# Where the tail of each stage is issued: merging the last four gated tiles together, deferring the first convolutions, and the last norm's factor in PSUM

## The chip, the cores and the metric

The kernel runs on one core of a Trainium2 chip. Its engines work from separate in-order queues: PE (TensorE) multiplies matrices into PSUM, DVE (VectorE) and ACT (ScalarE) do elementwise work, POOL (GpSimd) a little of it, and SP and ACT issue the DMAs. The metric is the device time of one execution in microseconds (us).

## The reference

One layer of a decoder trunk, 1024 tokens of 1024 channels, float32. What matters here:

```python
u = _modulate(h, g_mix, sh1, sc1)                 # RMSNorm, scale, shift; sh, sc, gt from silu(c) @ w_ada
y_att, y_ssm = ...                                # windowed attention and S5 branch, each projected to 1024
merged = sigmoid(g_att + gb_att) * y_att + sigmoid(g_ssm + gb_ssm) * y_ssm
h = h + gt1 * (merged @ w_out)
u = _modulate(h, g_ffn, sh2, sc2)
a, val = split(u @ w_up)                          # 2 x 2048 channels
conv = b_conv + sum(w_conv[j] * shift(a, j) for j in range(3))
h = h + gt2 * ((silu(conv) * val) @ w_down)
return _rmsnorm(h, g_final)
```

## The kernel before

Activations lie channels by tokens in tiles of 128 channels; the tokens fall in two halves (hf 0 and 1) of 512. Every matrix operand is kept as a high part in the PE's fast float format and a low part (the rest): ACT copies the high part, DVE (or POOL) subtracts to get the low part, and each product is three matmuls of 128x512 (`mm3`). A "group" is one output tile of 128x512: 8 k-tiles, 24 matmuls, for a contraction over 1024 channels; 2 k-tiles, 6 matmuls, for the projection of the S5 branch.

The order of work is written by a Python builder that keeps a clock of its own. Each k-tile calls `unit(0.65)`, which advances that clock and resumes background generators (`spawn`) that are due; what they issue then goes onto the engines' queues at that place. `drain()` runs background generators to their end, one after the other. So the builder's clock sets only the order on each queue; the chip sets the times.

The merge stage follows `merge_order`: "g" items are the gates of the S5 branch (two groups of 24 matmuls over u, then a sigmoid on ACT, L737), "p" items project two tiles (four groups of 6 matmuls, PSUM tags "s" and "t" of two banks each) and merge them on DVE: multiply by the gate (L757), add the attention part (L758), ACT's high part (L759), and the low part (L762), which is issued one group later through `lows`. Meanwhile `gen_ada` loads 16 rows of w_ada on ACT's queue (L772) and reduces each with a dot product on DVE (L1459), three buffers in turn. Ahead of the last "p" item the builder drains it. `Weights` loads and splits the next weights (L118 on ACT, L121 on DVE) into one of two `whl` buffers or, for some of the later ones, into the big pool A of 17 tiles, in which u, the gates and the merged tiles live too. A pool's tile is free when the last instruction that reads it is done.

Then w_out is multiplied (8 groups per half, `residual` adds to h, L882, and gathers the squares for the norm). The up projection's first pair of tiles is done as plain groups (8 groups: kind 0 the convolved part, kind 1 the value part, e = 0 in tag "s", e = 1 in tag "mm"); the rest of the up projection and the down projection are Strassen products M1 to M7 of 12 matmuls (L1305). During those first groups `gen_u2b` norms the second half of the tokens (L897, L902, L865, L869) and forms the differences T1, T2, T3, T4 of the quarters (L937 to L940). `block` takes a group's result: for kind 0 ACT scales it (L1015) and DVE adds the two shifted copies (L1022) and the edge (L1010); for kind 1 DVE multiplies (L1004).

At the end each half's last norm is a generator `final`: PE sums the squares (L1418, L1420), ACT (L1427, L1429) and DVE (L1431, L1432) form the factor in `acc`, and DVE (L1405, L1407) and POOL (L1407) multiply the eight tiles by it; SP stores them (L1409, L1412). The second half comes in two pieces of 256 tokens.

Of the kernel before, what the change touches and what calls it, by code (L numbers as in the profile page):

```python
# [10 lines left out]
F32 = mybir.dt.float32  # L11
# [30 lines left out]
ADA1 = 8.0  # L42
FIN = 5.0
PREP = 4
# [25 lines left out]
class Weights:  # L70
# [25 lines left out]
    def _split_to(self, n):  # L96
        b, nc = self.b, self.b.nc
        while self.ns < min(n, len(self.items)):
            self.finish()
            self._load_to(self.ns + 1)  # L100
            cols = self.items[self.ns][1]
            raw = self.raw.pop(self.ns)
            if self.ns >= self.small and ((self.ns - self.small) % 3 == 0 or self.wide + 2 <= self.ns < self.wide + 4 or
                                          self.ns >= len(self.items) - 2):
# [38 lines left out]
class Builder:  # L143
# [65 lines left out]
def body(tc, I, O, dbg=None):  # L209
    b = Builder(tc, I, O)  # L210
    nc = tc.nc
    with ExitStack() as ctx:
# [516 lines left out]
        def gate_ssm(m, wg):  # L729
            if m % 2 == 0:  # L730
                page = b.A([P, 2, S], F32, "sg")
                sgs[m], sgs[m + 1] = page[:, 0], page[:, 1]
            sig = sgs[m]
            for hf in range(2):
                ps = b.ps("mm")
                b.run(b.group(ps, wg, KT, U, hf))
                nc.scalar.activation(sig[:, hf * HF:(hf + 1) * HF], ps, AF.Sigmoid,  # L737
                                     bias=cols[:, C_BGATE + KT + m:C_BGATE + KT + m + 1])

# [4 lines left out]

        def proj_ssm(m0, wp, more):

            for e in range(2):
                merged.append(b.A([P, 2, S], R32, "merged"))
            for hf in range(2):
                hs = slice(hf * HF, (hf + 1) * HF)  # L750
                for e in range(2):
                    m = m0 + e
# [4 lines left out]
                    nc.vector.tensor_mul(t, ps, t)  # L757
                    nc.vector.tensor_add(t, t, Tm[m // 2][:, m % 2, hs])  # L758
                    nc.scalar.activation(mt[:, 0, hs], t, AF.Copy)  # L759
# [4 lines left out]
            del sgs[m0], sgs[m0 + 1]  # L764

# [39 lines left out]
        for n, it in enumerate(merge_order):  # L805
# [112 lines left out]
        def gen_u2b():  # L918

            v = nc.vector  # L920
            hs = halves[1]
# [5 lines left out]
            op_new("22")  # L927
            x11, x12, x21, x22 = [[X[q, e][:, k] for k in range(4)] for q in range(2) for e in range(2)]
            xs2 = [("12", k, x12[k]) for k in range(4)] + [("22", k, x22[k]) for k in range(4)]
            for n in range(KT + LAG2):  # L930
# [4 lines left out]
            op_new("T2")  # L935
            for k in range(4):
                v.tensor_sub(x11[k], x12[k], x11[k])  # L937
                v.tensor_sub(x12[k], x22[k], x12[k])
# [57 lines left out]
        def block(r, kind, e, hf, src):  # L996

            m = r + e * FT // 2
            c = page[r][:, e, halves[hf]]
            if kind == 1:  # L1000
                if r:
                    shifted.append(lambda: nc.vector.tensor_mul(c, src, c))
                else:
                    nc.vector.tensor_mul(c, src, c)  # L1004
                return
# [384 lines left out]
        assert not early and not lag and not older  # L1390
        b.drain()


def final(b, hv, hf, acc, ends, hs, cols, O):
    nc = b.nc
    rms_of(b, acc[:, hs], ends.pop(hs.start))
    yield 0.5
    cs = slice(hs.start - hf * HF, hs.stop - hf * HF)
    for m0 in (6, 0, 2, 4):
        out = b.A([P, 2, 256], F32, "out") if hf else None  # L1400
        for m in (m0 + 1, m0):
            x = hv[m, hf][:, cs]
            o = out[:, m - m0] if hf else x
            if m == KT - 1 or hf and m == ND - 1:
                nc.vector.scalar_tensor_tensor(o, x, cols[:, C_GFIN + m:C_GFIN + m + 1], acc[:, hs], op0=OP.mult, op1=OP.mult)  # L1405
            else:
                (nc.gpsimd if m in FPOOL[hf] else nc.vector).tensor_mul(o, x, acc[:, hs])  # L1407
# [15 lines left out]

def rsqrt_of(b, r, ps):

# [5 lines left out]
    nc.vector.scalar_tensor_tensor(t, ps, -EPS * D, t, op0=OP.add, op1=OP.mult)  # L1431
    nc.vector.scalar_tensor_tensor(r, t, 1.5, r, op0=OP.add, op1=OP.mult)  # L1432

# [512 lines left out]
```

## Time and profile before

| | |
|---|---|
| time, median of 3 runs | 1157.44 us (1157.3 to 1157.76) |
| the profiled execution | 1157.34 us, span from first to last instruction 1155.4 us |
| mean granted PE clock | 0.986 |
| busy: PE, DVE, ACT, POOL | 96%, 76%, 50%, 13% of the span |

In the rows below, a timeline row gives start, duration, engine, line and operation, output and inputs, the count of merged instructions, and in brackets the idle time before it with what ended it. A row of a list of waits gives the total, the number and the longest. A row of windows gives start:end and length, busy time and count of PE, PE's weight load, DVE, ACT and POOL, then the granted clock of PE, the share of the DMA engines and GB/s.

### The profile page before, as it was taken

The numbers are of one execution on the slowest core, as the hardware profiler recorded it, in microseconds if no ns is written. First come the engines' busy times: TensorE is split into PE (matmuls) and PEld (weight loads), VectorE is DVE, ScalarE is ACT, GpSimd is POOL, SyncE is SP. The second block draws the span as 40 slices with busy tenths as digits, with TensorE's granted clock in tenths as the row PEclk, the third lists the DMA queues.
The fourth block names the chain that finished last, engine by engine and source line by source line (L and its number), as shares of the span: only waits on it lengthen the run. The fifth ranks groups of instructions, "written<-read, shape, count | busy, mean of one in ns | idle before, by whom it ended". The sixth has DMA issues, their size and how long they took to land.

```text
span 1155.4 us, 14755 instructions
## 1 busy us (share of the span) xinstructions
PE 1112.6 (96%) x5286; PEld 917.2 (79%) x5286; DVE 872.6 (76%) x1672; ACT 581.8 (50%) x1062; POOL 150.2 (13%) x171
## 2 busy tenths in 40 slices
PE   9899999999999999999799998999999999999995
PEld 8677888888878887888688886788888888887884
DVE  6678687876568597378767779888877768889777
ACT  3648777778732312242334565452445346736653
POOL 1001444545421312000000000000000000000003
PEclk9899999999999999999899999999999999999997
DMA  9811111111022221146592342255424337779333
GB/s 370 343 55 70 49 38 37 56 37 65 17 75 73 57 87 51 64 140 195 166 381 81 120 201 73 91 175 190 143 76 146 109 109 272 257 293 343 129 126 146
DMA packets 57337, 159.20 MB, mean 138 GB/s; under 512 B 7440, under 2 KB 13712, under 8 KB 55472
## 3 DMA queue, kind: packets, MB, share of 16 engines
q1 hardware_dynamic: 47520, 144.56, 35.1%
q10 hardware_dynamic: 9744, 13.70, 3.7%
q8 instruction: 41, 0.67, 0.2%
q14 instruction: 32, 0.26, 0.1%
HBM read 126.20 MB, written 31.46 MB: 136 GB/s over the span
## 4 chain that ended last, share of the span: by engine, by line
PE 66%; DVE 15%; ACT 8%; DMA 7%; issue 3%; POOL 0%; SPq 0%; DVEq 0%; ACTq 0%
PE ps_s L1305 13%; PE ps_mm L1305 10%; PE ps_t L1305 8%; PE ps_mm L184 6%; PE ps_mm L185 6%; PE ps_mm L186 6%; PE ps_s L186 3%; PE ps_s L184 3%; PE ps_s L185 3%; DMA xn<-in_xn 2%; PE ps_t L1598 2%; PE ps_s L1562 1%; PE ps_o L1615 1%; PE ps_s L1563 1%; DMA wraw<-in_w 1%
## 5 line engine op out<-in xcount | busy, mean ns | idle before, releaser
L1305 PE MATMUL ps_s<-op,half 128*128 128x512 f32 x792 | 189.5, 390 | 3.0 <-ACT ps_s L1319 2.4
L1305 PEld LDWEIGHTS ps_s<-op,half 128*128 128x128 f32 x792 | 148.4, 188 | 35.4 <-ACT ps_s L1319 3.8
L184 PE MATMUL ps_mm<-u,whl 128*128 128x512 f32 x360 | 145.0, 403 | 3.1 <-ACT sg L737 2.0
L186 PE MATMUL ps_mm<-u,whl 128*128 128x512 f32 x360 | 141.6, 393 | 0.0
L185 PE MATMUL ps_mm<-u,whl 128*128 128x512 f32 x360 | 141.4, 393 | 0.0
L1305 PE MATMUL ps_mm<-op,half 128*128 128x512 f32 x528 | 126.9, 393 | 3.0 <-DVE f L1010 2.8
L1305 PEld LDWEIGHTS ps_mm<-op,half 128*128 128x128 f32 x528 | 99.7, 189 | 24.6 <-ACT half L1110 3.2
L1305 PE MATMUL ps_t<-op,half 128*128 128x512 f32 x432 | 103.9, 390 | 0.7 <-ACT tp L1313 0.7
L1305 PEld LDWEIGHTS ps_t<-op,half 128*128 128x128 f32 x432 | 81.0, 188 | 17.9 <-ACT tp L1313 1.1
L1407 POOL TENSOR_TENSOR hh<-hh,acc 128x512 f32<-128x512 f32 x3 | 4.2, 1439 | 652.1 <-DVE acc L1432 652.1
L121 POOL TENSOR_TENSOR whl<-wraw,whl 128x256 fp32r<-128x256 f32 (+2 forms) x52 | 62.0, 1193 | 207.8 <-ACT whl L118 207.8
L184 PEld LDWEIGHTS ps_mm<-u,whl 128*128 128x128 f32 x360 | 68.1, 189 | 15.3 <-ACT sg L737 2.5
L186 PEld LDWEIGHTS ps_mm<-u,whl 128*128 128x128 f32 x360 | 68.0, 189 | 15.3 <-DVE whl L121 0.3
L185 PEld LDWEIGHTS ps_mm<-u,whl 128*128 128x128 f32 x360 | 68.3, 190 | 10.5
L1603 DVE TENSOR_TENSOR PT<-ps_t,PT 128x512 fp32r<-128x512 f32 (+1 forms) x80 | 50.6, 633 | 28.2 <-ACT PT L1601 27.7
L1111 DVE TENSOR_TENSOR half<-scr,half 128x512 fp32r<-128x512 f32 x80 | 54.5, 685 | 16.2 <-ACT half L1110 16.1
L118 ACT ACTIVATE whl<-wraw 128x256 fp32r<-128x256 f32 (+2 forms) x73 | 49.7, 681 | 28.3 <-PE ps_s L186 14.6
L1574 ACT ACTIVATE S<-S,mcol 128x128 f32<-128x128 f32 (+3 forms) x64 | 49.3, 771 | 14.5 <-DVE mcol L1572 13.0
L1578 POOL TENSOR_SCALAR S<-S,mcol 128x128 f32<-128x128 f32 (+3 forms) x64 | 48.6, 761 | 49.9 <-DVE mcol L1577 35.9
L1110 ACT ACTIVATE half<-scr 128x512 fp32r<-128x512 f32 x80 | 49.0, 626 | 8.6 <-DVE scr L1092 5.5
L1111 DVE TENSOR_TENSOR half<-wraw,half 128x512 fp32r<-128x512 f32 x66 | 45.0, 686 | 7.6 <-ACT half L1110 7.5
L1601 ACT ACTIVATE PT<-ps_t 128x512 fp32r<-128x512 f32 (+1 forms) x80 | 43.7, 550 | 10.4 <-PE ps_t L1598 9.3
(507 smaller groups left out, 2438.0 us busy)
## 6 DMA issues: line engine op xcount, KB each, us to landing
wraw<-in_wup SPq DMA_DIRECT2D x32, 512.0 KB, 3.7
fq<-f SPq DMA_DIRECT2D x16, 1024.0 KB, 5.4
ft<-fq SPq DMA_DIRECT2D x14, 1024.0 KB, 7.5
ada<-in_wada SPq DMA_DIRECT2D x24, 512.0 KB, 8.7
wraw<-in_wdn SPq DMA_DIRECT2D x20, 512.0 KB, 5.9
adaB<-in_wada ACTq DMA_DIRECT2D x16, 512.0 KB, 4.9
wraw<-in_wout SPq DMA_DIRECT2D x16, 512.0 KB, 3.9
hd<-h SPq DMA_DIRECT2D x12, 512.0 KB, 7.9
```

Source lines behind the costliest of these rows:

```text
L118: nc.scalar.activation(w[:, 0, cs], raw[:, cs], AF.Copy)
L121: lo.tensor_sub(w[:, 1, cs], raw[:, cs], w[:, 0, cs].bitcast(F32))
L184: nc.tensor.matmul(ps, wh, xh, start=first, stop=False)
L185: nc.tensor.matmul(ps, wh, xl, start=False, stop=False)
L186: nc.tensor.matmul(ps, wl, xh, start=False, stop=last)
L1110: nc.scalar.activation(w[:, 0], src, AF.Copy)
L1111: lows.append(lambda: nc.vector.tensor_sub(w[:, 1], src, w[:, 0].bitcast(F32)))
L1305: mm = lambda wp, xp, i: nc.tensor.matmul(ps, w[:, wp, ws], xp[:, cs], start=first and k + i == 0, stop=k == KT // 2 - 1 and i == 2, skip_ ...
L1574: nc.scalar.activation(tl, tl, AF.Exp, bias=mc[:, 0:1], scale=-1.0, accum_out=mc[:, 2:3])
L1578: nc.gpsimd.tensor_scalar(tl, tl, mc[:, 3:4], 0.0, op0=OP.mult, op1=OP.add)
L1601: nc.scalar.activation(pt[:, 0, :w], tps[:, :w], AF.Copy)
L1603: 0, lambda: nc.vector.tensor_sub(pt[:, 1, :w], tps[:, :w], pt[:, 0, :w].bitcast(F32)))
```

## The change

Four parts. In the merge stage, the order ends "g7 p4 p6" instead of "p4 g7 p6": p4's weights are held, and its two tiles and p6's two are projected and merged together after g7, over three PSUM tags, with the drain ahead of all four; the second w_out weight goes to pool A. The gate's sigmoid is issued at its last k-tile, ahead of what the background issues there. In the first up groups, the shifts and the multiplications on DVE become background tasks 2.0 of the clock later, and the differences are formed two k-tiles at a time. In `final`, the factor goes to a PSUM tile for DVE, ACT copies it to `acc` for POOL, the first half's outputs are issued 1.4 apart instead of 0.5, and the generators left at the end take turns.

```diff
-FIN = 5.0
+FIN, OUT_PACE, FIRST = 5.0, 1.4, 2.0
...
-            if self.ns >= self.small and ((self.ns - self.small) % 3 == 0 or self.wide + 2 <= ...
+            if self.ns >= self.small and ((self.ns - self.small) % 3 == 0 or self.ns == self.small + 1 or self.wide + 2 <= ...
...
+    def take_turns(self):
+        while self.bg:
+            for t in list(self.bg):
+                if next(t[0], None) is None:
+                    self.bg.remove(t)
...
-        merge_order = "g0 g1 g2 g3 glu g4 p0 g5 p2 g6 p4 g7 p6".split()
+        merge_order = "g0 g1 g2 g3 glu g4 p0 g5 p2 g6 g7 p4 p6".split()
...
-                b.run(b.group(ps, wg, KT, U, hf))
-                nc.scalar.activation(sig[...], ps, AF.Sigmoid, ...)
+                for n, us in enumerate(b.group(ps, wg, KT, U, hf)):
+                    if n == KT - 1:
+                        nc.scalar.activation(sig[...], ps, AF.Sigmoid, ...)
+                    b.unit(us)
...
-        def proj_ssm(m0, wp, more):
+        def proj_ssm(todo, tags, between=None):
...
             for hf in range(2):
-                for e in range(2):
-                    ps = b.ps("t" if e else "s")
-                    b.run(b.group(ps, wp, 2, Z, hf, e * 256))
+                for m, wp, c0 in todo:
+                    ps = b.ps(tags[n % len(tags)])
+                    n += 1
+                    b.run(b.group(ps, wp, 2, Z, hf, c0))
                     ...                      # L757, L758, L759, lows as before
-                more()
+                if between:
+                    between()
...
-                if n == len(merge_order) - 1:
+                m = int(it[1])
+                if m < 4:
+                    W.prefetch(iw + n + 2)
+                    proj_ssm(two(m, w), "st")
+                elif m == 4:
+                    held = two(m, w)
+                else:
                     b.drain()
                     load_h(0)
                     load_h(1)
-                W.prefetch(iw + n + 2)
-                proj_ssm(int(it[1]), w, lambda: W.prefetch(iw + n + 3) if n == len(merge_order) - 1 else None)
+                    W.prefetch(iw + n + 2)
+                    proj_ssm(held + two(m, w), ("s", "t", "mm"), lambda: W.prefetch(iw + n + 3))
...
             op_new("T2")                     # in gen_u2b
-            for k in range(4):
-                v.tensor_sub(x11[k], x12[k], x11[k])
-                ...                          # x12, x22, x21; op_hi of k, op_lo of k - 1
-                yield T2P
+            for kk in range(2):
+                ks = slice(2 * kk, 2 * kk + 2)
+                for o, x, y in ((x11, x12, x11), (x12, x22, x12), (x22, x22, x11), (x21, x21, x22)):
+                    nc.vector.tensor_sub(o[:, ks], x[:, ks], y[:, ks])
+                    if o is x22:
+                        for k in (2 * kk, 2 * kk + 1):
+                            op_hi("T2", k, x22[:, k])
+                op_lo2("T2", kk, x22)        # both low parts in one instruction; more_lo likewise
+                yield 2 * T2P
...
-                    nc.vector.tensor_mul(c, src, c)
+                    b.spawn(once(mult), FIRST)
...
-                shifts()
+                b.spawn(once(shifts), FIRST)
...
-        b.spawn(spill(0, page.pop(0)), SP0)
+        b.spawn(spill(0, page.pop(0)), SP0 + FIRST)
...
-        b.drain()
+        b.take_turns()
...
 def final(b, hv, hf, acc, ends, hs, cols, O):
-    rms_of(b, acc[:, hs], ends.pop(hs.start))
+    ...                                      # the same matmuls on PE
+    root = rsqrt_of(b, acc[:, hs], ps, b.ps("s")[:, :n])
+    next(root)                               # ACT's two steps
+    yield 0.5
+    r = next(root)                           # DVE's two steps, the factor r in PSUM
+    nc.scalar.activation(acc[:, hs], r, AF.Copy)
     yield 0.5
...
-                nc.vector.scalar_tensor_tensor(o, x, cols[...], acc[:, hs], op0=OP.mult, op1=OP.mult)
+                nc.vector.scalar_tensor_tensor(o, x, cols[...], r, op0=OP.mult, op1=OP.mult)
+            elif m in FPOOL[hf]:
+                nc.gpsimd.tensor_mul(o, x, acc[:, hs])
             else:
-                (nc.gpsimd if m in FPOOL[hf] else nc.vector).tensor_mul(o, x, acc[:, hs])
+                nc.vector.tensor_mul(o, r, x)
             if not hf:
                 nc.sync.dma_start(O["outT"][m][:, hs], o)
-                yield 0.5
+                yield OUT_PACE
```

More of the change, by code (lines that the diff above doesn't have):

```diff
@@ L102, in _split_to @@
             raw = self.raw.pop(self.ns)
[L103 removed]
+            if self.ns >= self.small and ((self.ns - self.small) % 3 == 0 or self.ns == self.small + 1 or self.wide + 2 <= self.ns < self.wide + 4 or
                                           self.ns >= len(self.items) - 2):
@@ L735, in gate_ssm @@
                 ps = b.ps("mm")
-                b.run(b.group(ps, wg, KT, U, hf))
-                nc.scalar.activation(sig[:, hf * HF:(hf + 1) * HF], ps, AF.Sigmoid,
-                                     bias=cols[:, C_BGATE + KT + m:C_BGATE + KT + m + 1])
+                for n, us in enumerate(b.group(ps, wg, KT, U, hf)):
+                    if n == KT - 1:
+                        nc.scalar.activation(sig[:, hf * HF:(hf + 1) * HF], ps, AF.Sigmoid,
+                                             bias=cols[:, C_BGATE + KT + m:C_BGATE + KT + m + 1])
+                    b.unit(us)
         def Z(k, hf):
@@ L743, in body @@
         lows = []
-        def proj_ssm(m0, wp, more):
-            for e in range(2):
+        def proj_ssm(todo, tags, between=None):
+            for m, _, _ in todo:
                 merged.append(b.A([P, 2, S], R32, "merged"))
+            n = 0
             for hf in range(2):
                 hs = slice(hf * HF, (hf + 1) * HF)
-                for e in range(2):
-                    m = m0 + e
+                for m, wp, c0 in todo:
                     mt = merged[m]
-                    ps = b.ps("t" if e else "s")
-                    b.run(b.group(ps, wp, 2, Z, hf, e * 256))
+                    ps = b.ps(tags[n % len(tags)])
+                    n += 1
+                    b.run(b.group(ps, wp, 2, Z, hf, c0))
                     t = sgs[m][:, hs]
@@ L762, in proj_ssm, with two @@
                     lows[:] = [lambda mt=mt, t=t, hs=hs: nc.vector.tensor_sub(mt[:, 1, hs], t, mt[:, 0, hs].bitcast(F32))]
-                more()
-            del sgs[m0], sgs[m0 + 1]
+                if between:
+                    between()
+            for m, _, _ in todo:
+                del sgs[m]
+        def two(m, w):
+            return [(m, w, 0), (m + 1, w, 256)]
         def gen_ada():
@@ L826, in body @@
                     load_h(1)
-                W.prefetch(iw + n + 2)
-                proj_ssm(int(it[1]), w, lambda: W.prefetch(iw + n + 3) if n == len(merge_order) - 1 else None)
+                    W.prefetch(iw + n + 2)
+                    proj_ssm(held + two(m, w), ("s", "t", "mm"), lambda: W.prefetch(iw + n + 3))
+                    del held
         b.drain()
@@ L869, in op_lo, with op_lo2 @@
             eng.tensor_sub(lo, src, hi.bitcast(F32))
+        def op_lo2(name, kk, page):
+            t = ops[name][kk]
+            nc.vector.tensor_sub(t[:, :, 1], page[:, 2 * kk:2 * kk + 2], t[:, :, 0].bitcast(F32))
         hd = [b.dram.tile([P, S], F32, name=f"hd{k}") for k in range(KT)]
@@ L927, in gen_u2b @@
             op_new("22")
-            x11, x12, x21, x22 = [[X[q, e][:, k] for k in range(4)] for q in range(2) for e in range(2)]
-            xs2 = [("12", k, x12[k]) for k in range(4)] + [("22", k, x22[k]) for k in range(4)]
+            x11, x12, x21, x22 = [X[q, e] for q in range(2) for e in range(2)]
+            xs2 = [("12", k, x12[:, k]) for k in range(4)] + [("22", k, x22[:, k]) for k in range(4)]
             for n in range(KT + LAG2):
@@ L950, in more_hi @@
             for k in range(4):
-                op_hi(name, k, diff[name][k])
+                op_hi(name, k, diff[name][:, k])
         def more_lo(name):
-            for k in range(4):
-                op_lo(name, k, diff[name][k], nc.vector)
+            for kk in range(2):
+                op_lo2(name, kk, diff[name])
         def gen_ada1(j0, pace):
@@ L1034, in block, with once @@
             else:
-                shifts()
+                b.spawn(once(shifts), FIRST)
+        def once(fn):
+            fn()
+            yield 0
         def spill(r, f):
@@ L1390, in body @@
         assert not early and not lag and not older
-        b.drain()
+        b.take_turns()
 def final(b, hv, hf, acc, ends, hs, cols, O):
     nc = b.nc
-    rms_of(b, acc[:, hs], ends.pop(hs.start))
+    n = hs.stop - hs.start
+    ps = b.ps("o")[:, :n]
+    gone = ends.pop(hs.start)
+    nc.tensor.matmul(ps, b.nones, acc[:, hs], start=True, stop=False)
+    for i, x in enumerate(gone):
+        nc.tensor.matmul(ps, b.nones, x, start=False, stop=i == len(gone) - 1)
+    del gone
+    root = rsqrt_of(b, acc[:, hs], ps, b.ps("s")[:, :n])
[3 more added lines that the diff above has]
+    nc.scalar.activation(acc[:, hs], r, AF.Copy)
     yield 0.5
@@ L1404, in final @@
             if m == KT - 1 or hf and m == ND - 1:
-                nc.vector.scalar_tensor_tensor(o, x, cols[:, C_GFIN + m:C_GFIN + m + 1], acc[:, hs], op0=OP.mult, op1=OP.mult)
+                nc.vector.scalar_tensor_tensor(o, x, cols[:, C_GFIN + m:C_GFIN + m + 1], r, op0=OP.mult, op1=OP.mult)
+            elif m in FPOOL[hf]:
+                nc.gpsimd.tensor_mul(o, x, acc[:, hs])
             else:
-                (nc.gpsimd if m in FPOOL[hf] else nc.vector).tensor_mul(o, x, acc[:, hs])
+                nc.vector.tensor_mul(o, r, x)
             if not hf:
                 nc.sync.dma_start(O["outT"][m][:, hs], o)
-                yield 0.5
+                yield OUT_PACE
         if hf:
@@ L1421, in rms_of, with rsqrt_of @@
     list(rsqrt_of(b, acc, ps))
-def rsqrt_of(b, r, ps):
+def rsqrt_of(b, r, ps, out=None):
     nc = b.nc
@@ L1431, in rsqrt_of @@
     nc.vector.scalar_tensor_tensor(t, ps, -EPS * D, t, op0=OP.add, op1=OP.mult)
-    nc.vector.scalar_tensor_tensor(r, t, 1.5, r, op0=OP.add, op1=OP.mult)
+    nc.vector.scalar_tensor_tensor(r if out is None else out, t, 1.5, r, op0=OP.add, op1=OP.mult)
+    yield out
 def mod_a(nc, hi, x, t, gs, r, sh):
```

11 lines of the change are left out of this document (2 added, 9 removed).

## The prediction

> **What bounds the kernel now.** I read the page first, then the list of waits of PE, then the timeline of PE, DVE and ACT where PE stops.
>
> ```profile
> PE 1112.6 (96%) x5286; PEld 917.2 (79%) x5286; DVE 872.6 (76%) x1672; ACT 581.8 (50%) x1062; POOL 150.2 (13%) x171
> ...
> PE ps_s L184 <- DVE sg L757: 5.0, 1, 5.0
> ...
> PE ps_mm L1305 <- DVE f L1010: 2.8, 1, 2.8
> PE ps_mm L1305 <- DVE hh L882: 2.8, 1, 2.8
> ...
> PE ps_mm L184 <- ACT sg L737: 2.0, 1, 2.0
> ```
>
> PE is busy 96% of 1155.4 us, so only its stops can be won, and whatever runs after its last matmul. Three of the four long stops above lie where the diff works: the end of the merge stage (5.0), the first Strassen product (2.8), the end (2.8). Each costs more than its wait:
>
> ```profile
> 567.60:573.90 6.30, 5.12 (x11) 3.60 (x12) 6.23 (x10) 2.84 (x4) 0.00 (x0) 0.51 0.36 122
> ...
> 1133.90:1141.20 7.30, 4.48 (x25) 4.49 (x26) 5.91 (x12) 2.99 (x5) 0.00 (x0) 0.77 0.44 169
> ```
>
> The third number from the right is the granted clock: about half for 6.3 us after the 5.0 us stop, and low again after the 2.8 us stop at the end.
>
> **Merge stage: the order "g7 p4 p6" and eight groups in a row.** PE, ACT, DVE rows of the old end of the stage, and how long gen_ada's loads take (least, median, most):
>
> ```profile
> 540.48 0.39 PE L184 MATMUL ps_s<-zsh,whl 128*128 128x512 f32 x1
> 562.22 0.39 PE L186 MATMUL ps_t<-zsh,whl 128*128 128x512 f32 x1
> 567.60 0.77 PE L184 MATMUL ps_s<-merged,whA 128*128 128x512 f32 x1 [5.00 <-DVE sg L757]
> 569.98 0.80 PE L186 MATMUL ps_s<-merged,whA 128*128 128x512 f32 x1 [1.18 <-DVE whA L121]
> 576.88 0.39 PE L184 MATMUL ps_mm<-merged,whl 128*128 128x512 f32 x1
> 582.32 0.39 PE L184 MATMUL ps_s<-merged,whl 128*128 128x512 f32 x1
> ...
> 552.23 1.15 ACT L759 ACTIVATE merged<-sg 128x512 fp32r<-128x512 f32 x2 [7.45 <-PE ps_mm L186]
> 555.49 0.62 ACT L118 ACTIVATE whl<-wraw 128x512 fp32r<-128x512 f32 x1
> 558.83 0.69 ACT L737 ACTIVATE sg<-ps_mm,cols 128x512 f32<-128x512 f32 x1 [1.06 <-PE ps_s L186]
> ...
> 556.58 0.69 DVE L121 TENSOR_TENSOR whl<-wraw,whl 128x512 fp32r<-128x512 f32 x1
> 565.62 1.23 DVE L1459 CUSTOM_DVE_ANT_0 adaB<-adaB,cs 128x1024 f32<-128x1024 f32 x1
> 566.77 0.69 DVE L757 TENSOR_TENSOR sg<-ps_s,sg 128x512 f32<-128x512 f32 x1
> 568.70 1.22 DVE L121 TENSOR_TENSOR whA<-wraw,whA 128x1024 fp32r<-128x1024 f32 x1
> 569.84 0.69 DVE L757 TENSOR_TENSOR sg<-ps_t,sg 128x512 f32<-128x512 f32 x1
> 571.77 0.68 DVE L757 TENSOR_TENSOR sg<-ps_s,sg 128x512 f32<-128x512 f32 x1
> ...
> DMA to landing us min/median/max: 3.4/4.9/6.7
> ```
>
> 24 matmuls take 582.32 - 576.88 = 5.44 us. Old: p4 at 540.48, g7, p6 to 562.4; then the drained dot products (last 565.62) stand before p6's L757 on DVE, PE waits for a PSUM bank, then for a weight split, then runs at half clock. New: g7 at 540.48 to 551.4, then eight groups of 1.36 us.
>
> What is better: the tile merged[5] no longer waits for g7's reading of u (ACT's 7.45). What is worse: p6's weights can be split only when g7's buffer is free, because p4's are held. The split (ACT 0.62, DVE 0.69) comes behind the last sigmoid (0.69): 551.5 + 2.0 = 553.4 on DVE. And gen_ada is drained 5.2 clock units earlier (its steps, due every 1.6, come every 1.95, as k-tiles of 0.65 count): five dot products, not three or four, stand ahead of all eight groups, and behind p6's split on DVE. Two of them (1.15 each) free the buffers of the last two loads, issued at 554.7 and 555.8. At the median of 4.9 the last dot product starts near 560.7; with h[0] and w_out also loading I take 561.3, so L757 begins at t0 = 562.4.
>
> A group costs DVE 1.93 (569.84 to 571.77: multiply, add, one subtraction). The first w_out tile needs the bank that the fourth group's multiply frees: t0 + 3 x 1.93 + 1.14 (a split) + 0.7 = 570.0. PE runs six groups on six banks to 559.6, two more in bits, stops, and starts there at half clock for up to 3.5 us: end 575.4 to 577.1, second tile's end 580.9 to 582.5. The third needs DVE's split behind all eight groups: t0 + 8 x 1.93 + 3 x 1.14 + 1.0 = 582.2. Old start of the third: 582.32. So **0**; by the shortest landing -2.2, by the longest with half clock +1.5. Putting w_out tile 1 in the big pool costs nothing: after g7 all eight tiles of u are free there. On SP the loads of h[0] and h[1] wait for gen_ada's last buffers and w_out tile 2 stands behind them; it is issued near 561 and wanted by ACT near 580, so its landing (4.9) is hidden, and if it were not, that would be its price.
>
> The clock row comes first: half rate from 567.6 to 573.9 after 5.0 us. [...]
>
> **Sigmoid with its last k-tile: 0.** It moves the sigmoid ahead of what the background issues at that one k-tile. gen_ada's loads on ACT fall due at 0.65 + 3.9n, the gates end at multiples of 5.2: in k-tiles 6n + 1 against 8m, never the same. The 2.0 us wait above is g0's sigmoid behind the S5 GELU, which is issued in the first four k-tiles of that gate, so it stays. Were it won, -2.0 and some half clock, -3.9.
>
> **Up projection, first tiles: convolutions deferred, T2 in pairs.**
>
> ```profile
> 673.21 1.53 DVE L1022 SCALAR_TENSOR_TENSOR f<-ps_s,cols,f 128x511 f32<-128x511 f32 x2 [1.93 <-ACT edge L1017]
> 682.71 1.53 DVE L1022 SCALAR_TENSOR_TENSOR f<-ps_mm,cols,f 128x511 f32<-128x511 f32 x2 [2.90 <-ACT edge L1017]
> 690.35 0.68 DVE L937 TENSOR_TENSOR x<-x 128x512 f32<-128x512 f32 x1
> 691.07 0.69 DVE L938 TENSOR_TENSOR x<-x 128x512 f32<-128x512 f32 x1
> 693.73 0.68 DVE L937 TENSOR_TENSOR x<-x 128x512 f32<-128x512 f32 x1
> 709.26 0.68 DVE L1111 TENSOR_TENSOR half<-scr,half 128x512 fp32r<-128x512 f32 x1
> 709.86 0.69 DVE L1004 TENSOR_TENSOR f<-ps_s,f 128x512 f32<-128x512 f32 x1
> ...
> 708.50 0.70 PE L1305 MATMUL ps_mm<-op,half 128*128 128x512 f32 x2 [2.83 <-DVE f L1010]
> 713.94 0.74 PE L1305 MATMUL ps_s<-op,half 128*128 128x512 f32 x2 [0.67 <-ACT ps_s L1319]
> ```
>
> DVE is the late engine: M1 waits from 705.7 for the bank of the sixth up group, then runs at half clock; M6 starts at 713.94. Deferral by 2.0 means the fourth k-tile of the next group. The two idle stretches before L1022 (1.93, 2.90) then hold norm2's work, tiles 3 and 4 before the first shifts, 5 to 8 before the second. Worked through instruction by instruction in the new order, one stretch of 2.0 is left of the 4.8, where DVE waits for ACT, which still has its table load there: -2.8. T2 costs 693.73 - 690.35 = 3.38 per k, 13.5 in all; a dependent step starts 0.72 after the last (L937 to L938), a free one 0.60 (709.26 to 709.86). On 1024 columns a free one takes 1.14 (568.70 to 569.84), a dependent one by the same 0.12 some 1.26: three of these, two of the others, 6.1 per pair, 12.1 (an estimate): -1.4. Against it, two L1111 of 0.60 now come before the sixth group's shifts: +1.2. The low parts of T1, T3 and T4 in pairs save 0.1 each, behind a DVE that then no longer sets PE's pace: 0. Bank free at 708.5 - 3.0 = 705.5, PE ready at 705.7, a11's low part long done. M1 then takes 2.72 at full clock plus the copy wait 0.67: M6 at 709.1, **-4.8**. Bounds: if the idle stretches stayed and only T2's part came, less the L1111 that then stands ahead, -0.8; below, nothing more than the stop can go, -4.9. SP's store of page 0 goes 2.0 later and its tile is not awaited before the sums, 17 units on.
>
> **The end.**
>
> ```profile
> 1124.45 0.69 DVE L1431 SCALAR_TENSOR_TENSOR tp<-ps_o,tp 128x512 f32<-128x512 f32 x1 [2.73 <-ACT tp L1429]
> 1126.45 0.74 DVE L882 SCALAR_TENSOR_TENSOR hh<-ps_mm,mod,hh 128x512 f32<-128x512 f32 x1
> 1129.11 1.77 DVE L1405 SCALAR_TENSOR_TENSOR hh<-hh,cols,acc 128x512 f32<-128x512 f32 x1
> ...
> 1136.72 2.72 PE L1305 MATMUL ps_mm<-op,sw 128*128 128x256 f32 x12 [2.82 <-DVE hh L882]
> ...
> 1141.98 0.48 DVE L882 SCALAR_TENSOR_TENSOR hh<-ps_t,mod,hh 128x256 f32<-128x256 f32 x1
> 1142.81 0.46 ACT L1427 ACTIVATE acc<-ps_o,epsc 128x256 f32<-128x256 f32 x1
> 1144.80 2.66 POOL L1407 TENSOR_TENSOR out<-hh,acc 128x256 f32<-128x256 f32 x3 [14.47 <-DVE acc L1432]
> 1145.76 6.95 SPq L1412 DMA_DIRECT2D outT<-out x8
> ```
>
> Now DVE idles 2.73 for ACT with a finished product behind it, and L1405 takes 1.77 while POOL runs; L882, one input in PSUM, stays at 0.74 beside the same POOL work. After: the yield lets that product's L1295 and L882 go first, OUT_PACE 1.4 leaves two outputs rather than five before the next L882, and the factor is in PSUM. L882 then frees PE's bank near 1132.7, PE asks at 1133.5: the 2.82 and the half clock behind it (window above) go. DVE is next: its own work up to the last L882 ends near 1139.4 instead of 1142.4, and ACT's root starts near 1140.2 instead of 1142.81: -2.6. On SP the eight outputs of the first half are issued over more time, which nothing behind them waits for. The rest: DVE's two pieces (1143.8 to 1152.3, one after the other) go in turn without POOL's toll, but POOL's six multiplications (0.89 each) now start 0.5 later behind ACT's copy and chain to 1148.6; the last issue is near 1149.5 instead of 1152.3. **-2.8**; ends 0 and -4.5 (all of PE's loss and 0.6 in turn).
>
> On the factor in PSUM the rows above decide. [...]
>
> **Sum.** 0 - 4.8 - 2.8 = -7.6. The profiled execution took 1157.34, 0.1 below the median: 1149.7 and 1149.8; I say 1149.7.
>
> **Rivals.** (a) One half fails: DVE still frees M1's bank late (only T2's 0.8): 1153.7; or the end keeps its wait because POOL's toll or ACT's copy eats it: 1152.5. For it: DVE is busy almost without a break in both places; against it: 0.2 us of margin at M1, 0.8 at the end. (b) Both fail: 1156.5, no change. (c) The merge stop closes too: if the drained loads were issued behind nothing, t0 near 553, the third w_out tile would start at 562.3 + 10.9 = 573.2, nine earlier: 1141; with half of that 1145. Against it: p6's split waits for g7's last matmul. (d) Slower: the half clock. PE gets twelve matmuls between 559.6 and 570.0; if the clock stays at 0.51 while w_out runs, each half tile costs 5.44 / 0.51 - 5.44 = 5.2 more. From the third such half tile on (15.6, less the 7.6 won) the kernel is slower: 1165. Against it: the old clock was back after 4 us of steady matmuls.
>
> **Chances.** Forecast 0.55 (its own range 1147.5 to 1152), (a) 0.20, (b) 0.10, (c) 0.08, (d) 0.07. The range takes forecast, (a) and the nearer part of (c): 1146 to 1154.5. Faster by over 0.2% (2.3 us, about what a measurement here can tell) 0.82, same 0.11, slower 0.07.
>
> **What would show it.** Merge: PE's stop before the first w_out matmul starting near 559.6, third w_out tile within 1.5 us of 582.3; a dot product ending near 562 before the first L757 of p4. Up: M1 directly behind the last up matmul, granted clock 1.0 there. End: no wait at p2's first product; outputs of both pieces alternating; POOL's six ending last. Wrong if the third w_out tile moves by more than 3 us, or M1 still waits over 1 us.

## The result and the profile after

The changed kernel takes 1150.95 us (median of 4 runs, 1149.02 to 1151.91) against 1157.6 (4 runs, 1157.3 to 1157.97): ratio 0.994, 95% interval 0.9923 to 0.9958. The prediction was 1149.7, with a range of 1146 to 1154.5. The profiled execution took 1151.12, its span is 1149.3 against 1155.4.

PE's list of waits after the change (total, number, longest):

```profile
PE ps_s L190 <- DVE sg L766: 6.0, 2, 3.7
...
PE ps_s L1333 <- ACT ps_s L1347: 2.9, 2, 2.1
PE ps_mm L190 <- ACT sg L744: 2.0, 1, 2.0
...
PE ps_mm L191 <- DVE zl L1890: 0.8, 1, 0.8
```

The two stops of 2.8 are gone. The merge stage still stops (5.0 has become 3.7 and 2.3), the wait ahead of M6 for ACT's copy of M1's sums into the PSUM tile on which M6 adds (L1319, now L1347; it is called the seed below, and the wait the copy wait) has grown from 0.67 to 2.1, and a wait of 0.8 for `zl` is new. Rows of the timeline, DVE and PE at the merge stage:

```profile
553.96 0.69 DVE L121 TENSOR_TENSOR whl<-wraw,whl 128x512 fp32r<-128x512 f32 x1 [7.07 <-ACT whl L118]
...
560.66 1.23 DVE L1502 CUSTOM_DVE_ANT_0 adaB<-adaB,cs 128x1024 f32<-128x1024 f32 x1 [2.57 <-DMA adaB<-in_wada]
562.61 1.22 DVE L1502 CUSTOM_DVE_ANT_0 adaB<-adaB,cs 128x1024 f32<-128x1024 f32 x1 [0.72 <-DMA adaB<-in_wada]
563.76 0.69 DVE L766 TENSOR_TENSOR sg<-ps_s,sg 128x512 f32<-128x512 f32 x1
...
582.62 1.22 DVE L121 TENSOR_TENSOR whl<-wraw,whl 128x1024 fp32r<-128x1024 f32 x1
...
564.51 0.79 PE L190 MATMUL ps_s<-zsh,whl 128*128 128x512 f32 x1 [3.66 <-DVE sg L766]
571.52 0.47 PE L190 MATMUL ps_s<-merged,whA 128*128 128x512 f32 x1 [2.29 <-DVE sg L766]
583.90 0.50 PE L192 MATMUL ps_s<-merged,whl 128*128 128x512 f32 x1 [0.54 <-DVE whl L121]
```

DVE idles 7.07 us beneath g7, then 2.57 and 0.72 at loads, and only then takes the first of eight groups; the third w_out tile waits for the split that stands behind them. The up stage and the end:

```profile
706.78 2.89 PE L1333 MATMUL ps_mm<-op,half 128*128 128x512 f32 x12
711.80 3.01 PE L1333 MATMUL ps_s<-op,half 128*128 128x512 f32 x12 [2.13 <-ACT ps_s L1347]
...
707.54 1.14 ACT L1138 ACTIVATE half<-scr 128x512 fp32r<-128x512 f32 x2
708.58 2.17 ACT L886 ACTIVATE op<-x 128x512 fp32r<-128x512 f32 x4
710.66 0.61 ACT L1138 ACTIVATE half<-wraw 128x512 fp32r<-128x512 f32 x1
711.18 0.57 ACT L1347 ACTIVATE ps_s<-ps_mm 128x512 f32<-128x512 f32 x1
...
1131.12 1.60 PE L1333 MATMUL ps_mm<-op,sw 128*128 128x256 f32 x12
...
1128.47 0.68 DVE L1449 TENSOR_TENSOR hh<-ps_s,hh 128x512 f32<-128x512 f32 x1
1137.81 0.46 ACT L1469 ACTIVATE acc<-ps_o,epsc 128x256 f32<-128x256 f32 x1
1140.14 4.42 POOL L1447 TENSOR_TENSOR out<-hh,acc 128x256 f32<-128x256 f32 x6 [10.44 <-ACT acc L1436]
1141.14 4.92 SPq L1454 DMA_DIRECT2D outT<-out  x8
```

M1 stands directly behind the up groups, p2's first product waits for nothing, ACT's root starts at 1137.81 instead of 1142.81, and POOL's six multiplications take 0.74 each.

To compare kernels, PE's time is cut at five places: the 2.0 us wait of g0 (code before it is the same in all), the start of the fourth w_out tile, M6's start, the first half's norm matmul (L1418; L1428 after), and the end of the span. Lengths in us, each the difference of two PE rows of the profiled execution:

| kernel | to g0's wait | to w_out tile 4 | to M6 | to the norm | to the end |
|---|---|---|---|---|---|
| before | 452.81 | 134.94 | 126.19 | 406.67 | 34.79 |
| after | 453.48 | 135.54 | 122.78 | 406.53 | 30.97 |
| e1_merge | 453.31 | 134.30 | 126.34 | 406.21 | 36.34 |
| e13_sig | 452.99 | 134.38 | 122.78 | 406.50 | 30.95 |
| e2_up | 452.50 | 134.77 | 122.78 | 406.16 | 34.89 |
| e8_seed | 452.86 | 135.32 | 121.32 | 406.29 | 31.01 |
| e3_end | 452.87 | 134.86 | 126.94 | 406.47 | 30.56 |
| e9_sbuf | 453.29 | 135.74 | 122.78 | 408.11 | 32.98 |
| e12_drain | 452.98 | 135.71 | 122.79 | 407.79 | 31.23 |
| e4_ada | 453.26 | 131.63 | 122.78 | 407.40 | 30.53 |
| e6_late | 453.51 | 134.63 | 122.82 | 407.10 | 31.04 |
| e7_old_late | 452.61 | 128.10 | 126.97 | 406.82 | 35.20 |
| e10_best | 453.10 | 128.08 | 121.34 | 406.22 | 30.96 |
| e11_best2 | 452.78 | 126.58 | 121.34 | 406.25 | 30.95 |

After less before: +0.67, +0.60, -3.41, -0.14, -3.82, together -6.1. The first column is the same code and lies between 452.50 and 453.51: the +0.67 is not the change's. Kernels that share a stage's code agree there within about 0.4 in the second column, 0.8 in the third and 0.5 in the fifth with the new end; the old end goes from 34.79 to 36.34. Part of this spread is the clock, as the last section shows: in the third column PE ran at half clock for 3.4 us in before (0.51 from 710.25 to 713.75), and in e3_end M1's twelve products took 5.53, where they take 2.89 after the change. The fourth column, code that no run touches, goes from 406.16 to 408.11. e12_drain's 407.79 has half clock at its start (0.50 from 713 to 716); the 408.11 of e9_sbuf has none (its 128x512 products there start 0.22 to 0.24 apart), and its cause is open.

### The profile page after: what moved, and what is told of

It reads as the page before. It is cut to its first block, busy times and chain, and to the rows that moved or that the text cites. A ratio compares the mean times of both kernels' runs of the same rounds, so it can differ in the third digit from the quotient of the medians.

```text
span 1149.3 us, 14742 instructions
## 1 busy us (share of the span) xinstructions
PE 1108.6 (96%) x5286; PEld 912.2 (79%) x5286; DVE 866.3 (75%) x1656; ACT 583.2 (51%) x1065; POOL 149.6 (13%) x171
## 4 chain that ended last, share of the span: by engine, by line
PE 62%; DVE 14%; DMA 8%; ACT 8%; issue 8%; POOL 1%; SPq 0%; POOLq 0%; ACTq 0%; DVEq 0%
PE ps_s L1333 10%; PE ps_mm L1333 9%; PE ps_mm L190 7%; PE ps_t L1333 7%; PE ps_mm L192 7%; PE ps_mm L191 7%; PE ps_s L192 2%; PE ps_s L190 2%; PE ps_s L191 2%; DMA xn<-in_xn 2%; PE ps_t L1641 2%; PE ps_s L1605 1%; PE ps_o L1658 1%; PE ps_s L1606 1%; DMA x<-in_xT 1%
## 5 line engine op out<-in xcount | busy, mean ns | idle before, releaser
L121 POOL TENSOR_TENSOR whl<-wraw,whl 128x256 fp32r<-128x256 f32 (+2 forms) x52 | 62.1, 1196 | 208.1 <-ACT whl L118 208.1
L191 PEld LDWEIGHTS ps_mm<-u,whl 128*128 128x128 f32 x360 | 68.3, 190 | 10.5
L118 ACT ACTIVATE whl<-wraw 128x256 fp32r<-128x256 f32 (+2 forms) x72 | 48.7, 676 | 28.3 <-PE ps_s L192 14.6
L1138 ACT ACTIVATE half<-scr 128x512 fp32r<-128x512 f32 x80 | 49.0, 625 | 8.7 <-DVE scr L1120 5.6
L1644 ACT ACTIVATE PT<-ps_t 128x512 fp32r<-128x512 f32 (+1 forms) x80 | 43.8, 551 | 10.5 <-PE ps_t L1641 9.4
```

The costliest lines, as they stand in the source:

```text
L118: nc.scalar.activation(w[:, 0, cs], raw[:, cs], AF.Copy)
L121: lo.tensor_sub(w[:, 1, cs], raw[:, cs], w[:, 0, cs].bitcast(F32))
L191: nc.tensor.matmul(ps, wh, xl, start=False, stop=False)
L1138: nc.scalar.activation(w[:, 0], src, AF.Copy)
L1644: nc.scalar.activation(pt[:, 0, :w], tps[:, :w], AF.Copy)
```

## The experiments

All ratios are to the kernel before, run on the same chip beside them.

**e1_merge: the merge order alone,** with `proj_ssm` over four tiles and the second w_out weight in pool A; the sigmoid as before.

```diff
-        merge_order = "g0 g1 g2 g3 glu g4 p0 g5 p2 g6 p4 g7 p6".split()
+        merge_order = "g0 g1 g2 g3 glu g4 p0 g5 p2 g6 g7 p4 p6".split()
```

> Only the merge order, the four last tiles together and the big buffer for w_out tile 1. Theory (the reordering trades the 9 us stop before the eight groups for one behind them): third w_out tile within 0.5 us of the old 582.3, whole kernel 1157.5 +- 1. Rival (the reordering wins about 2 us here and the whole change loses it again through some shift of buffers): third w_out tile near 580, kernel near 1155.5.

Ratio 1.0001 (0.9991 to 1.0011). Tile 4 comes 0.6 earlier by the table (134.30 against 134.94, and 134.77 and 134.86 in e2_up and e3_end, which share that code): the order is worth about -0.5. The third tile itself came at 581.21, 1.1 ahead of 582.32, so my bound of 0.5 on it was missed; but it then stops for 0.54 at its weight split, which the old one did not.

**e13_sig: the changed kernel with the sigmoid issued as before.**

```diff
-                for n, us in enumerate(b.group(ps, wg, KT, U, hf)):
-                    if n == KT - 1:
-                        nc.scalar.activation(sig[...], ps, AF.Sigmoid, ...)
-                    b.unit(us)
+                b.run(b.group(ps, wg, KT, U, hf))
+                nc.scalar.activation(sig[...], ps, AF.Sigmoid, ...)
```

> The changed kernel with the sigmoid issued after its last k-tile, as before. The prediction's 0 for this edit: ratio 0.994 as the changed kernel, the 2.0 us wait of the first gate for the sigmoid unchanged, third w_out tile within 0.5 us of 582.6. Rival (the earlier issue moves the sigmoid ahead of a load or a GELU somewhere): the 2.0 us wait grows or 1 us or more is lost.

Ratio 0.9933 (0.9921 to 0.9945): its interval overlaps the changed kernel's, but the table does not leave it open. To tile 4 it takes 134.38, as e1_merge does; the four kernels with the new sigmoid, the new order and the dots where the change has them take 135.32 to 135.74. My 0 is wrong and the rival named there right: the sigmoid edit costs about 1.2. 0.9 of it is there when PE comes to its stop behind the groups (107.37 us after g0's wait, 106.48 in e13_sig). The rest lies in the length of that stop, which goes from 3.40 to 3.82 among three runs of the same merge code (e8_seed, after, e12_drain). The rows after the change, on ACT, DVE and PE:

```profile
486.21 0.69 ACT L744 ACTIVATE sg<-ps_mm,cols 128x512 f32<-128x512 f32 x1 [4.23 <-PE ps_mm L192]
486.80 1.05 ACT L1884 ACTIVATE gw<-gw 128x1024 f32<-128x1024 f32 x1
...
491.22 2.00 DVE L1890 TENSOR_TENSOR zl<-z,zh 128x1024 fp32r<-128x1024 f32 x1 [2.11 <-ACT zh L1889]
...
493.28 0.50 PE L191 MATMUL ps_mm<-zl,whl 128*128 128x512 f32 x1 [0.75 <-DVE zl L1890]
```

and with the old sigmoid (e13_sig):

```profile
485.38 1.06 ACT L1882 ACTIVATE gw<-gw 128x1024 f32<-128x1024 f32 x1 [3.88 <-DVE gw L1881]
487.73 2.04 ACT L1887 ACTIVATE zh<-z 128x1024 fp32r<-128x1024 f32 x1 [1.29 <-DVE z L1883]
489.68 0.68 ACT L743 ACTIVATE sg<-ps_mm,cols 128x512 f32<-128x512 f32 x1
...
489.81 2.04 DVE L1888 TENSOR_TENSOR zl<-z,zh 128x1024 fp32r<-128x1024 f32 x1 [2.11 <-ACT zh L1887]
```

A GELU of the S5 branch (`gw`, not the one that g0 waits for) falls due in the last k-tile of that gate. Issued earlier, the gate's sigmoid waits 4.23 for its matmuls at the head of ACT's queue, and the GELU, whose input was ready, stands behind it: 1.42 later (0.49 of it is the two runs' offset at g0), and so `z`, `zh` and `zl`, for which PE then waits 0.75. The trace of the kernel before has this GELU too, at 485.54 on ACT, ahead of that gate's sigmoid at 489.85. The wait is in every trace with the new sigmoid and in none with the old one.

**e2_up: the deferred convolutions and T2 in pairs alone.**

```diff
-                    nc.vector.tensor_mul(c, src, c)
+                    b.spawn(once(mult), FIRST)
...
-                shifts()
+                b.spawn(once(shifts), FIRST)
...                                           # and T2, more_lo in pairs
```

> Only the deferred first convolutions and the T2 differences in pairs. Theory (M1 starts without a wait, the rest is taken by a copy wait of 2.1 before M6, ACT having T3's and a22's work ahead of the seed): M6 near 710.5 instead of 713.9, kernel 1154.1, that is -3.4. Rival (the copy wait comes from the shift of the merge stage and not from this part): the wait stays 0.67, M6 at 709.1, kernel 1152.7, that is -4.8.

Ratio 0.9978 (0.9968 to 0.9988). M6 at 710.05, the copy wait 2.10: the theory's numbers, and 122.78 to M6, the same as after. The rival's -4.8 would be 0.9959, outside the interval. So the wait of 2.1 belongs to this part. In the rows after the change ACT has two L1138, T3's four copies (2.17) and a22's L1138 ahead of the seed L1347; M1's products are finished at 709.67 and the seed starts at 711.18.

**e8_seed: T3's copies one step later.**

```diff
-MORE = (0, 1, 2)
+MORE = (1, 1, 2)
```

> The changed kernel with T3's four fp32r copies issued one step later (MORE 1, 1, 2 instead of 0, 1, 2), so that they stand behind the seed on ACT's queue. Theory (ACT's order makes the seed late: 2.2 us of T3 copies ahead of it): the copy wait before M6 falls from 2.13 to 0.7, M6 1.4 earlier, and all behind it; ratio near 0.993 where the changed kernel has 0.994. Rival (M7 or M5 then wait for T3's or T1's low part and take it back): M3 no earlier than in the changed kernel.

Ratio 0.9923 (0.991 to 0.9935). Rows of PE and ACT:

```profile
705.95 2.88 PE L1333 MATMUL ps_mm<-op,half 128*128 128x512 f32 x12
709.50 3.06 PE L1333 MATMUL ps_s<-op,half 128*128 128x512 f32 x12 [0.67 <-ACT ps_s L1347]
...
708.86 0.58 ACT L1347 ACTIVATE ps_s<-ps_mm 128x512 f32<-128x512 f32 x1 [0.48 <-PE ps_mm L1333]
709.36 4.27 ACT L886 ACTIVATE op<-x 128x512 fp32r<-128x512 f32 x8
```

The seed waits for PE again and not for ACT's queue; the stage is 1.46 shorter than after (121.32 against 122.78), and M3, which comes behind the products that read T3 and T1, starts at 721.40, 15.45 after M1 instead of 16.88. Nothing is given back.

**e3_end: the end alone.**

```diff
+    r = next(root)
+    nc.scalar.activation(acc[:, hs], r, AF.Copy)
...                                           # OUT_PACE 1.4
-        b.drain()
+        b.take_turns()
```

> Only the end: factor in PSUM, outputs spaced by 1.4, the last pieces in turn. Theory (PE's 2.8 us stop and its half clock go, -2.7, and the tail behind PE's end is 1.1 shorter because POOL's multiplications cost 0.74 and not 0.89): kernel 1153.7, that is -3.8. Rival (the tail's gain rests on the earlier stages): -2.8 or less, 1154.7.

Ratio 0.9958 (0.9944 to 0.9971); 30.56 to the end against 34.79 before, 30.97 in the full change. The theory's -3.8 (0.9967) lies in the interval; the rival's -2.8 (0.9976) lies outside it. So the gain of the tail does not rest on the earlier stages.

**e9_sbuf: the factor left in SBUF, all else as changed.**

```diff
-    root = rsqrt_of(b, acc[:, hs], ps, b.ps("s")[:, :n])
+    root = rsqrt_of(b, acc[:, hs], ps)
...
-    r = next(root)
-    nc.scalar.activation(acc[:, hs], r, AF.Copy)
+    next(root)
+    r = acc[:, hs]
```

> The changed kernel with the last norm's factor left in SBUF as before (no PSUM bank for it, no ACT copy), so that DVE's last multiplications read two SBUF operands beside POOL's. Theory (the two engines slow each other only when DVE reads two SBUF operands: DVE 1.77 against 0.75, POOL 0.90 against 0.74): DVE's multiplications beside POOL near 1.7 for 512 columns, POOL's 256-column ones back at 0.89, p2's second half waits again, last store issue 2 to 3 us later: kernel 2.5 us over the changed one, ratio 0.996. Rival (the order of the turns and the spacing brought it, the place of the factor nothing): within 0.5 us of the changed kernel, ratio 0.994.

Ratio 0.9958 (0.9945 to 0.9972). DVE and POOL rows:

```profile
1129.97 1.78 DVE L1449 TENSOR_TENSOR hh<-acc,hh 128x512 f32<-128x512 f32 x1
...
1144.61 1.80 DVE L1449 TENSOR_TENSOR out<-acc,hh 128x256 f32<-128x256 f32 x2
...
1142.42 0.73 POOL L1447 TENSOR_TENSOR out<-hh,acc 128x256 f32<-128x256 f32 x1 [11.22 <-DVE acc L1474]
1143.56 4.30 POOL L1447 TENSOR_TENSOR out<-hh,acc 128x256 f32<-128x256 f32 x5 [0.41 <-DVE acc L1474]
```

DVE's 512-column product takes 1.78 beside POOL, where it takes 0.68 with the factor in PSUM (1128.47 above), and POOL's take 0.86 (4.30 / 5) instead of 0.74; POOL's first, with no DVE product beside it, took 0.73. The end is 2.0 longer (32.98 against 30.97). What I got wrong: p2's second half waits only 0.26 and 0.36 here, so PE's 2.8 us stop went by the order and spacing of the outputs, not by the factor's place.

**e12_drain: the last two pieces one after the other.**

```diff
-        b.take_turns()
+        b.drain()
```

> The changed kernel with the last two norm pieces drained one after the other, as before, instead of in turn. Theory (of the 3.8 at the end 2.0 come from the factor in PSUM and 2.7 of the rest from PE's stop; the turns alone let the second piece's root and factor overlap the first piece's multiplications): last store issue 1 to 2 us later, ratio 0.995. Rival (DVE's and POOL's work is the tail in either order): ratio 0.994, within 0.3 us.

Ratio 0.9943 (0.993 to 0.9956), 31.23 to the end against 30.97: the turns are worth about 0.3, which is less than kernels with the whole new end differ among themselves (30.53 to 31.04). The rival is right: with the factor in PSUM the tail is the same work in either order.

**e4_ada: the modulation loads and dots paced at 1.2 instead of 1.6.**

```diff
-                yield 1.6                    # in gen_ada, both places
+                yield 1.2
```

> The changed kernel with the modulation loads and dot products of the merge stage paced at 1.2 instead of 1.6 units, so that none is left to drain ahead of the eight groups. Theory (the five drained dot products, the last near 563, set when the first product of the eight groups starts, and through DVE's 15 us of work behind it the third w_out tile): first product near 555, third w_out tile near 574.5 instead of 582.6, kernel 1142.5. Rival (DVE's work for eight groups or the weight splits bind as much as the dots): third w_out tile after 579.5, kernel above 1147.5, a gain under 3.

Ratio 0.9914 (0.9899 to 0.9928). The stage is 3.9 shorter than after, not 8: the third w_out tile starts at 579.36 and the kernel takes 1148.55, close to the rival's numbers, not the theory's. PE's stops behind g7 are gone, but there is a new one at 534.55. DVE, ACT and PE:

```profile
529.05 1.23 DVE L1502 CUSTOM_DVE_ANT_0 adaB<-adaB,cs 128x1024 f32<-128x1024 f32 x1 [2.96 <-DMA adaB<-in_wada]
...
533.28 1.22 DVE L121 TENSOR_TENSOR whl<-wraw,whl 128x1024 fp32r<-128x1024 f32 x1
...
530.75 1.06 ACT L118 ACTIVATE whl<-wraw 128x1024 fp32r<-128x1024 f32 x1 [3.56 <-DVE mod L1502]
...
534.55 0.50 PE L192 MATMUL ps_mm<-u,whl 128*128 128x512 f32 x1 [1.95 <-DVE whl L121]
```

A dot product issued sooner waits for its load at the head of DVE's queue, with the products of p2 and the next weight split behind it. On ACT's queue the next load, which needs that dot's buffer, is issued at 530.32, and the weight's copy (L118, 530.75) stands behind it. The wait was moved, not removed.

**e6_late: the drain and the loads of h[0] and h[1] between the first four groups and the last four.**

```diff
-                    b.drain()
-                    load_h(0)
-                    load_h(1)
+                    def between():
+                        if not h:
+                            b.drain()
+                            load_h(0)
+                            load_h(1)
+                        W.prefetch(iw + n + 3)
+
                     W.prefetch(iw + n + 2)
-                    proj_ssm(held + two(m, w), ("s", "t", "mm"), lambda: W.prefetch(iw + n + 3))
+                    proj_ssm(held + two(m, w), ("s", "t", "mm"), between)
```

> The changed kernel, with the drain of the modulation dot products and the loads of h[0] and h[1] moved from ahead of the eight groups to between the first four and the last four; the pace stays 1.6. Theory (DVE idles 3.3 us at loads in front of products that stand finished in PSUM, and this idle time is what is lost; the work itself has to be done either way): first product near 556 instead of 563.8, third w_out tile near 579.5 instead of 582.6, no stop of PE over 2 us before w_out, kernel 3 us under the changed one: 1.0 to 1.1% under before in time, ratio near 0.991. Rival (DVE's 25 us of work in this stretch is the bound wherever the dots stand): third tile within 1 us of 582.6, ratio 0.994.

Ratio 0.9934 (0.9921 to 0.9948): 0.9 in the stage, not 3, and the third w_out tile at 581.75: the rival's numbers. The first product comes at 555.79, as expected, but the stop only moves:

```profile
565.37 0.34 ACTq L786 DMA_DIRECT2D adaB<-in_wada  x1
...
570.60 1.23 DVE L1506 CUSTOM_DVE_ANT_0 adaB<-adaB,cs 128x1024 f32<-128x1024 f32 x1 [2.43 <-DMA adaB<-in_wada]
571.75 0.69 DVE L766 TENSOR_TENSOR sg<-ps_t,sg 128x512 f32<-128x512 f32 x1
...
573.82 0.73 PE L191 MATMUL ps_s<-merged,whA 128*128 128x512 f32 x1 [3.86 <-DVE merged L771]
```

The last load needs the buffer of a dot that ends at 563.9; its issue then stands on ACT's queue behind the fourth group's high part (565.30), and it lands 5 us later, again ahead of products. That DVE still idles 2.43 for it speaks against the rival's reason, that DVE's work alone is the bound.

**e7_old_late: the same late drain in the old order,** between the halves of p6, nothing else changed.

> The kernel before, unchanged but for the same late drain, between the two halves of p6. It asks whether the new merge order is needed for it. Theory (the dots in front of p6's first product are the stop, not the order): first product of p6 near 559 instead of 566.8, third w_out tile near 578.5 instead of 582.3, kernel 3 to 4 us under before, ratio 0.997. Rival (in the old order the tile merged[5] waits for g7's reading of u, so p6 and w_out stay where they are): ratio 1.000 +- 0.0005.

Ratio 0.9948 (0.9935 to 0.996), the stage 6.8 shorter than before (128.10 against 134.94), twice the theory's guess:

```profile
557.34 1.23 DVE L1463 CUSTOM_DVE_ANT_0 adaB<-adaB,cs 128x1024 f32<-128x1024 f32 x1
558.49 0.69 DVE L757 TENSOR_TENSOR sg<-ps_s,sg 128x512 f32<-128x512 f32 x1
...
565.78 1.22 DVE L1463 CUSTOM_DVE_ANT_0 adaB<-adaB,cs 128x1024 f32<-128x1024 f32 x1
566.92 0.69 DVE L757 TENSOR_TENSOR sg<-ps_s,sg 128x512 f32<-128x512 f32 x1
...
569.00 0.50 PE L185 MATMUL ps_s<-merged,whA 128*128 128x512 f32 x1 [2.45 <-DVE merged L762]
569.99 0.69 DVE L757 TENSOR_TENSOR sg<-ps_t,sg 128x512 f32<-128x512 f32 x1
```

No dot waits for a load (all are issued by 559.95), PE's stops of 5.00 and 1.18 become one of 2.45, and no half clock follows it (granted clock 1.00 from 569 to 574); that is about the other half of the gain, and it is the less certain half, since waits of 2.05 and 2.13 were followed by half clock in some traces and not in others (last section). By the ratio the gain is 6.0. So the stop needed the drain moved and not the order changed. In the new order the same drain gave 0.9 (e6_late). The likely reason is that this order puts p4's four groups, which DVE did beneath g7, behind g7 (the 7.07 us idle above), and needs gen_ada's end 5.2 units sooner; that is argued, and a drain behind all eight groups of the new order was not run.

**e10_best and e11_best2: put together.** Old merge order and sigmoid, late drain, the new up stage with `MORE = (1, 1, 2)`, the new end; e11_best2 drains behind all four groups of p6.

```diff
-                    if not h:
+                    k[0] += 1                # called after each half
+                    if k[0] == 2:
                         b.drain()
                         load_h(0)
                         load_h(1)
```

> The old merge order with the late drain, the new up-projection stage with T3's copies one step later, the new end; without the new merge order and without the sigmoid edit. Theory (the four places are independent, so their gains add: -6.0 as measured for the late drain in the old order, -3.5 up stage, -1.4 seed, -3.8 end): 14.7 under before, ratio 0.987, third w_out tile near 576, copy wait before M6 0.7. Rival (the earlier merge stage leaves later loads or DVE work behind, which take some of it back): ratio 0.990 or more.

> As the run before it, but the drain and the loads of h[0] and h[1] behind all four groups of p6. Theory (PE's last stop there, 2.45 us at the second half's low parts behind three dot products, goes): third w_out tile 2 us earlier still, ratio 0.985. Rival (h[0], h[1] and the w_out tile queued behind them on SP are issued 5 to 6 us later, and the weight split that already waited 0.85 us for its load waits that much longer): the gain is given back at the third or fourth w_out tile, ratio 0.987 or more.

e10_best: 1142.35 us, ratio 0.9868 (0.9856 to 0.9881): the gains add. e11_best2: 1140.24 us, ratio 0.9849 (0.9836 to 0.9861), the stage another 1.5 shorter, and the loads of h[0] and h[1], now issued from 568.26, came in time. PE there waits for one split alone:

```profile
574.23 0.50 PE L192 MATMUL ps_s<-merged,whl 128*128 128x512 f32 x1 [0.59 <-DVE whl L121]
```

It beats both kernels: 17.6 us under before, and by the two ratios about 10.5 under the change.

## Why the prediction was right, point by point

The sum was 0 - 4.8 - 2.8 = -7.6. Measured by stages it is +0.6 - 3.4 - 0.1 - 3.8, and +0.7 that is not the change's: -6.1. Two terms came out 1.2 and 1.4 worse than forecast (the sigmoid, the up stage), two 0.5 and 1.0 better (the order, the end); they cancel in part, so some of the closeness of the total is luck.

- **Merge stage, 0: -0.5, its mechanism right.** Five dots stand ahead of eight groups and behind p6's split; the last ends at 563.8 and L766 starts there (t0 said 562.4, the trace is 0.67 late at g0 and about 0.9 more by the sigmoid); first w_out tile at 571.5 (said 570.0), third at 582.6 (said 582.2). PE's stop began at 564.51 - 3.66 = 560.85 (said 559.6). The half clock that I put into w_out fell into the groups (0.50 from 564.0 to 567.4), where PE waits anyway. Its length of up to 3.5 us in the sum is taken from no row; the traces of before and after show 3.4 or 6.8.
- **Sigmoid, 0: +1.2, wrong.** The step that failed is "the sigmoid ahead of what the background issues": I compared its k-tile with gen_ada's loads alone. The S5 GELU is background too, and the prediction names it for g0 only.
- **Up stage, -4.8: -3.4.** Deferral and pairs did what they should: M1 directly behind the last up matmul at full clock (1.00 from 706 to 710). The mis-sized term is "the copy wait 0.67": 2.13. The prediction watched DVE, the late engine of the old trace, and not what stands on ACT ahead of the seed once DVE is early; T3's copies had been hidden beneath M1, which its stop and the half clock made late: in the kernel before they end at 712.58 on ACT, M1's products at 713.27. With them behind the seed the stage loses 4.85, the sum as written.
- **End, -2.8: -3.8.** ACT's root came 5.0 earlier, 2.7 of it after the norm matmul's own shift of 2.28 (said 2.6). From the root to the end of the span it is 12.59 before and 11.49 after, -1.1 where I had -0.2: I let POOL's six keep their 0.89 while DVE lost its toll; they took 0.74, and 6 x 0.15 = 0.9. The place of the factor gives 2.0 and the turns about 0.3; the rest, about 1.5, is left to spacing and order, which were not run alone.
- **The rivals.** (a), (b) and (d) did not come. (c), the merge stop closing too, was put at 0.08 for this order and did not come; it was to be had in the old order.

## What to carry to other kernels

An edit that moves an instruction ahead on an in-order queue has to be priced by what then stands behind it: the sigmoid and T3's copies each cost 1.2 to 1.5 us although ACT is busy for only half of the span. When the late engine of a stage is made early, read the next engine's queue at the same place, instruction by instruction. And when a stop comes from work that waits for loads at a drain, try to move the drain behind the products that are ready before rearranging the products. It has to be tried: the same move gave 6.8 us of the stage in the old order and 0.9 in the new one, where the last load went out late.

## What the runs showed of the hardware

The clock. In a row of windows the granted clock is third from the right. The changed kernel ran at half clock, 0.50 from 564.0 to 567.4, behind PE's stop of 3.66 us:

```profile
564.00:566.00 2.00, 1.49 (x4) 1.21 (x5) 1.97 (x4) 0.63 (x1) 0.00 (x0) 0.50 0.29 119
```

Shorter stops are another matter. Behind the copy wait of 2.13 us, shown above for the changed kernel, its clock stayed at 1.00 (first row); behind the same wait in e12_drain it was halved:

```profile
713.00:716.00 3.00, 3.00 (x14) 2.47 (x14) 3.00 (x4) 2.01 (x5) 0.00 (x0) 1.00 0.87 275
...
711.48 4.26 PE L1333 MATMUL ps_s<-op,half 128*128 128x512 f32 x12 [2.13 <-ACT ps_s L1347]
713.00:716.00 3.00, 3.00 (x9) 2.33 (x8) 3.00 (x3) 0.77 (x3) 0.00 (x0) 0.50 0.85 304
```

The wait of g0, 2.04 or 2.05 us in every trace, is followed by half clock in eight of the fourteen and not in the other six: the 128x512 products behind it start 0.43 apart in the eight and 0.23 in the six. The kernel before is one of the eight:

```profile
452.81 0.51 PE L184 MATMUL ps_mm<-u,whl 128*128 128x512 f32 x1 [2.04 <-ACT sg L737]
454.50:457.50 3.00, 3.00 (x9) 2.33 (x8) 2.92 (x4) 0.00 (x0) 2.24 (x1) 0.50 0.00 0
```

Half clock followed the stops of 2.82 at the end of before and e2_up, of 2.83 ahead of M1 in before and e3_end, of 3.39 to 3.89 in the merge stage of after, e1_merge, e6_late, e9_sbuf, e12_drain and e13_sig, and of 5.00 to 5.49 in that of before, e2_up and e3_end. It did not follow those of 2.29 (after, e13_sig), 2.33 (e3_end), 2.45 (e7_old_late) and 2.47 (e10_best). So at 2.05 and at 2.13 us the length of a stop does not decide it, and what does is not shown. In the traces of before and after such a half clock lasted 3.4 us (before: 454.3 to 457.7, 710.3 to 713.8 and 1137.0 to 1140.4) or 6.8 (567.0 to 573.8, behind the stop of 5.00), and began 2.3 to 4.7 us after the stop had begun.

POOL beside DVE. With the factor in PSUM, POOL's 256-column product fell from 0.89 to 0.74 and DVE's toll went; e9_sbuf brought both back, to 0.86 and 1.78. So beside POOL DVE's 512-column product took 1.77 and 1.78 with both inputs in SBUF and 0.68 with one of them in PSUM. The PSUM input itself costs DVE no time that the rows show: 0.68 is what L1407 took before with both inputs in SBUF, once POOL had ended its three products (first row), and L757 with its PSUM input took the same 0.69 as L121 without one (566.77 and 556.58 in the prediction's rows).

```profile
1126.09 4.24 POOL L1407 TENSOR_TENSOR hh<-hh,acc 128x512 f32<-128x512 f32 x3 [652.12 <-DVE acc L1432]
...
1130.81 0.68 DVE L1407 TENSOR_TENSOR hh<-hh,acc 128x512 f32<-128x512 f32 x1
```
